# Sample attention handles two cached pieces per visit of TensorE instead of one, in a one-core decoder step

## The chip, the cores and the metric

The kernel runs on one core of a Trainium2 chip. The metric is the device time in microseconds of one execution. Three runs of the kernel before gave 2272.2 us in the median (2270.72 to 2273.8).

## The reference

One layer of a hybrid decoder, for 512 prompt tokens and 8 sample sequences of 4 new tokens each, model width 2048, everything in float32:

```python
h = rmsnorm(x); [q | k | v | u] = h @ w_in
A = dilated sliding-window attention on (q, k, v)     # 16 heads x 64
B = multi-scale causal pooling on u
x = x + concat(A, B) @ w_out
x = x + SwiGLU(rmsnorm(x));  y = rmsnorm(x)
```

The part that matters here is attention for the sample tokens, where each sequence has a cache of 2048 keys and values:

```python
kcat = jnp.concatenate([ck, k], axis=1); vcat = jnp.concatenate([cv, v], axis=1)
kg, vg = kcat[:, idxc], vcat[:, idxc]                 # gathered by stride
logits = jnp.einsum('bthd,btkhd->bhtk', q, kg) * scale + bias
p = jax.nn.softmax(logits, axis=-1)
out = jnp.einsum('bhtk,btkhd->bthd', p, vg)
```

Of the cached positions only 896 can be reached by any of the four queries (`NK` = 896, seven tiles of 128); with the 32 new tokens there are `NL` = 928 columns of logits, held as two halves of `HL` = 464.

## The kernel before

Everything is transposed: channels on partitions, the 544 tokens (512 prompt, 32 sample) along the free dimension. A projection is computed one tile of 128 output channels at a time: 16 steps over the input channels (`kt`), in each of which `mm3` (L193 to L199) issues six matmuls of 272 columns, since every float32 product is made of three products of rounded high and low parts. The weights come through a stream (`Stream`, L115): a DMA of 256 KB for four steps (L129), rounded by ScalarE (L143) and subtracted by VectorE (L148) ahead of use.

Attention is woven into the projections. `project` yields after every step, and after each yield `tick` (L765) is called, which may run a piece of prompt attention and a piece of sample attention; what these issue lands in program order between the six matmuls of one step and those of the next. `clock["d"]` counts the ticks. There are 48 for each of the eight head pairs `hp` (q, k and v tiles), from 48 on, and then 16 for each of eight u tiles.

Sample attention is a generator per group `g` of four heads, `sample_steps` (L574), appended when `hp` = 1, 3, 5, 7 is done, so it can first run in ticks 97, 193, 289 and 385. For each half `kh` of the keys it issues one bias matmul (`btH`), then for each of four `bl` (one sequence of each half of the batch) four matmuls L588, one per 32 output partitions, which read a piece of cached keys, and then two more bias matmuls (`btL`, `selR`) and a bare `yield`. Then come the softmax (VectorE, ScalarE, with bare yields between) and two rounds of transposes. After that for each `j` of seven cached tiles of values and one of new values there are four matmuls L635. Each group so reads eight pieces of keys and seven of values.

The pieces (928, 864 or 1024 KB) lie in `NBUF` = 3 buffers. `load_piece` (L406) is called after the matmuls of a piece, and issues the DMA (L413) of the piece three further on, into the buffer just read; so that DMA waits for those matmuls. It goes out on SyncE's queue (SP), which issues in program order, and which the weights of the projections (L129) and all small transfers use too.

What sets the pace is the counter `clock["s"]`. In each tick the loop at L777 runs the generator on as long as the counter is below `(d - 96) * 64 / 352`. A `yield 1` adds one to the counter and the loop goes on; a bare `yield` (r = 0) ends the loop for this tick; the end of the generator (r = -1) takes it off the queue and also adds one. While no group is queued the target goes on rising. After the sixth u tile's start (tick 480) whatever is left is run to its end.

Of the kernel before, what the change touches and what calls it, by code (L numbers as in the profile page):

```python
# [163 lines left out]
def program(ctx, tc, a):  # L164
    nc = tc.nc
# [128 lines left out]
    with pool("st", side="right") as sp:  # L294
# [41 lines left out]
        for u in range(NU):  # L336
            wq, wk = ws.take(), ws.take()
            for i in range(UW):
# [12 lines left out]
                if kt == 8:  # L351
                    fps = pS.tile([P, 512], F32, tag="S", name="fps")
                    for h in range(2):
                        nc.tensor.matmul(fps[h * 32:h * 32 + H, :320], rb33, c33[:, 320 * h:320 * h + 320], start=True,
                                         stop=True)
# [29 lines left out]
    loaded = deque()  # L385
# [11 lines left out]
    qz = [at.tile([P, 2, 160], F32, name=f"qz{i}") for i in range(4)]  # L397
# [8 lines left out]
    def load_piece():  # L406
        n = state["n"]
        if n < len(pieces) and len(loaded) < NBUF:
            src = pieces[n]
            t = kvp[0].tile([P, PIECE], F32, tag="kv", name="kv", bufs=NBUF)  # L410
            w = src.shape[1] * src.shape[2]
            v = t[:, :w].rearrange("p (c k) -> p c k", c=src.shape[1])
            dma(v, src)  # L413
            loaded.append(v)
            state["n"] = n + 1
# [158 lines left out]
    def sample_steps(g):  # L574
        ps = pS.tile([P, 2, 512], F32, tag="samp", name="SS")
        par = [(2 * g + hpl) % 4 for hpl in range(2)]
        for kh in range(2):
            o = ps[:, kh, :HL]
            ks = slice(kh * HL, (kh + 1) * HL)
            nc.tensor.matmul(o, btH[:, g], bohR[:, ks], start=True, stop=False, skip_group_check=True)  # L580
            if kh:
                for c in range(4):
                    nc.tensor.matmul(ps[32 * c:32 * c + 32, 1, NK1:HL], qd[par[c // 2]][:, c % 2],
                                     kn[par[c // 2]], start=False, stop=False, skip_group_check=True)
            for bl in range(4):
                kv = loaded.popleft()
                for c in range(4):
                    nc.tensor.matmul(ps[32 * c:32 * c + 32, kh, :kv.shape[2]],  # L588
                                     qz[par[c // 2]][:, c % 2, 32 * bl:32 * bl + 32], kv[:, c],
                                     start=False, stop=False, skip_group_check=True)  # L590
                load_piece()
                yield 1
            nc.tensor.matmul(o, btL[:, g], bohR[:, ks], start=False, stop=False, skip_group_check=True)
            nc.tensor.matmul(o, selR, browR[:, ks], start=False, stop=True, skip_group_check=True)
            yield
        yield
        sm = at.tile([P, 4], F32, name="sm", tag="sms", bufs=2)
        prob = at.tile([P, NL], F32, name="sprob", tag="sprob")
        nc.vector.tensor_reduce(sm[:, 0:1], ps[:, :, :HL], axis=AX.XY, op=ALU.max)
        nc.vector.tensor_scalar(sm[:, 1:2], sm[:, 0:1], -1.0, None, op0=ALU.mult)  # L600
        yield
        nc.scalar.activation(prob.rearrange("p (a b) -> p a b", a=2), ps[:, :, :HL], AF.Exp, bias=sm[:, 1:2],
                             accum_out=sm[:, 2:3])
        yield
        yield
        nc.vector.reciprocal(sm[:, 3:4], sm[:, 2:3])
        nc.vector.tensor_scalar(prob, prob, sm[:, 3:4], None, op0=ALU.mult)
        yield
        yield
        ptr = at.tile([P, NJ, P], F32, name="ptr", tag="ptr")  # L610
        for half in range(2):
            pt = pS.tile([P, 4, P], F32, tag="T", name="tps")
            for jj in range(4):
                j = 4 * half + jj
                if j < NJ:
                    nc.tensor.transpose(pt[:, jj], prob[:, j * P:(j + 1) * P], ident)
                else:
                    nc.tensor.transpose(pt[:NS, jj], prob[:, j * P:], ident)
            if half == 0:
                nc.vector.tensor_copy(ptr[:, :4], pt)  # L620
            else:
                nc.vector.tensor_copy(ptr[:, 4:], pt[:, :3])
                nc.vector.tensor_copy(pt7[:NS], pt[:NS, 3])
            yield
        pot = pS.tile([P, 2, 512], F32, tag="samp", name="SO")
        po = pot[:, 0]
        for j in range(NJ + 1):
            kv = loaded.popleft() if j < NJ else None
            for c in range(4):
                l = (ptr[:, j] if j < NJ else pt7)[:, 32 * c:32 * c + 32]  # L630
                if j < NJ:
                    r = kv.rearrange("p c (b f) -> p c b f", b=DB)[:, c // 2, 4 * (c % 2):4 * (c % 2) + 4]
                else:
                    r = vn[par[c // 2]][:, None, :].to_broadcast([P, 4, P])
                nc.tensor.matmul(po[32 * c:32 * c + 32, :].rearrange("p (b f) -> p b f", b=4), l, r,  # L635
                                 start=(j == 0), stop=(j == NJ), skip_group_check=True)
            if j < NJ:
                load_piece()
            yield 1
        vm = at.tile([P, 4, P], F32, name="vm", tag="vm")  # L640
        yield
        nc.vector.tensor_mul(vm, po.rearrange("p (b f) -> p b f", b=4), vmask)
        for _ in range(3):
            yield
        for b in range(4):
            nc.tensor.matmul(pot[:, 1, :64], vm[:, b], sel64, start=(b == 0), stop=(b == 3))
        m = at.tile([P, 64], F32, name="ms", tag="ms")
        nc.vector.tensor_copy(m, pot[:, 1, :64])
        for hpl in range(2):
            dma(mixd[2 * g + hpl][:, SEQ:], m[:, 32 * hpl:32 * hpl + 32])  # L650
        yield
# [93 lines left out]
    def run(gen, n=10 ** 6):  # L745
        r = 0
        for _ in range(n):
            r = next(gen, -1)
            if r == -1:
                return -1  # L750
        return r or 0
# [8 lines left out]
    clock = {"d": SPAN, "s": 0, "p": 0}  # L760
# [4 lines left out]
    def tick(lo, hi):  # L765

        clock["d"] += 1
        d = clock["d"]
        if d < S_FROM and d % 3 == 0:
            run(setup, 1)  # L770
        if d == S_FROM:
            run(setup)
        while prompt and clock["p"] < (d - lo) * P_STEPS / (hi - lo):
            clock["p"] += 1
            if run(prompt[0], 1) < 0:
                prompt.pop()
        while samples and clock["s"] < (d - S_FROM) * S_STEPS / (S_TO - S_FROM):  # L777
            r = run(samples[0], 1)
            if r < 0:
                samples.popleft()  # L780
            elif r == 0:
                break
            clock["s"] += 1

    for hp in range(8):
        for out in (q_out, k_out, v_out):
            acc = accv
            if hp:
                acc = acc_tile()
                for _ in project(acc):  # L790
                    tick(SPAN * hp, SPAN * hp + SPAN - 2)
            if hp or out is v_out:
                out(hp, acc)
        finish(prompt)
        clock["p"] = 0
        spread(hp)
        prompt.append(prompt_steps(hp))
        if hp % 2:
            samples.append(sample_steps(hp // 2))
# [26 lines left out]
    for n, ft in enumerate(u_order):  # L826
# [15 lines left out]
        for i, _ in enumerate(project(acc)):  # L842
            tick(8 * SPAN, 8 * SPAN + 3 * KT)
            if pools and run(pools[0], 1) < 0:
                pools.popleft()
            if staged and i % 2 and (n > 6 or i > 5):
                mix_in(*staged.popleft())
                mix_load()
# [183 lines left out]
    for n, nt in enumerate(nts):  # L1032
        load_x2(n + 1)
        acc = acc_tile()
        for u in range(NU):
            wh, wl, _ = ws.next()
# [7 lines left out]
            for i in range(UW):  # L1044
                j = UW * u + i
# [167 lines left out]
    for ci, (c0, n) in enumerate(chunks[:-1]):  # L1213
        groups = parts.pop(ci)
        ahead = load_g(ci + 1)
        for nt in range(KT):
# [3 lines left out]
            for u in range(n // UW):  # L1220
                if ci == nt == 0:
                    run(g0, 10 ** 6 if u == n // UW - 1 else 2)
                wh, wl, _ = ws2.next()
# [24 lines left out]
    for h in range(2):  # L1248
        c = slice(h * HALF, (h + 1) * HALF)
        for nt in range(KT):  # L1250
# [6 lines left out]
            for i in range(UW):  # L1257
                j = nt % 4 * UW + i
# [77 lines left out]
```

## Time and profile before

| | us |
|---|---|
| median of three runs | 2272.2 |
| the profiled execution | 2272.66 |
| its span, first to last instruction | 2270.9 |
| TensorE matmuls busy | 2236.9 (99%) |
| weight loads busy | 2143.0 (94%) |
| VectorE busy | 1387.8 (61%) |
| ScalarE busy | 851.9 (38%) |

The profiled execution has 1.8 us outside its span. Busy times are of one engine each and overlap; a matmul's end is modelled, so that consecutive matmuls overlap on the page and the time between two starts is what a matmul costs. A float32 matmul of the sample part shows as two records, so four of them stand as x8.

### The profile page before, as it was taken

How to read it: one execution, taken by the hardware profiler on the slowest of the kernel's cores; microseconds unless marked ns; L12 is line 12 of the kernel's file. 1: busy time of each engine (PE TensorE's matmuls, PEld its weight loads, DVE VectorE, ACT ScalarE, POOL GpSimd, SP SyncE). 2: the span in 40 equal slices, each digit the busy share in tenths (PEclk: the TensorE clock that was granted, in tenths of full speed). 3: DMA queues.
4: the chain of work that ended last, by engine and by line, in shares of the span. 5: the costliest groups of instructions: out<-in, count | busy, mean ns of one | idle time of the engine just before them, and what ended most of it. 6: DMA issues, size and time to landing. Idle time of an engine off the chain costs nothing.

```text
span 2270.9 us, 43394 instructions
## 1 busy us (share of the span) xinstructions
PE 2236.9 (99%) x17540; PEld 2143.0 (94%) x17540; DVE 1387.8 (61%) x2659; ACT 851.9 (38%) x1621; POOL 3.6 (0%) x28
## 2 busy tenths in 40 slices
PE   8999999999999999999999999999999999999997
PEld 8878787879999999999999999999999999999997
DVE  7644445476544688877878878887785333323256
ACT  6322222223333454444444444444444222222235
POOL 0000000000000000000000000000000000000000
PEclk9999999999999999999999999999999999999998
DMA  6666656676444432342343343333335533332233
GB/s 195 198 220 203 224 200 233 204 207 156 139 126 135 149 124 92 115 132 96 111 132 100 107 132 106 105 128 112 104 109 168 165 116 114 123 103 89 85 112 108
DMA packets 158693, 316.71 MB, mean 139 GB/s; under 512 B 28747, under 2 KB 34011, under 8 KB 154908
## 3 DMA queue, kind: packets, MB, share of 16 engines
q1 hardware_dynamic: 158112, 313.77, 43.4%
q8 instruction: 137, 2.24, 0.4%
q14 instruction: 64, 0.52, 0.1%
q10 hardware_dynamic: 380, 0.18, 0.0%
HBM read 284.32 MB, written 29.56 MB: 138 GB/s over the span
## 4 chain that ended last, share of the span: by engine, by line
PE 95%; DVE 2%; DMA 1%; ACT 1%; issue 1%; SPq 0%; DVEq 0%; ACTq 0%
PE acc L197 16%; PE acc L198 15%; PE acc L199 15%; PE X L973 8%; PE X L972 8%; PE X L974 8%; PE Z L973 4%; PE Z L972 4%; PE Z L974 4%; PE Y L973 2%; PE Y L972 2%; PE Y L974 2%; PE SO L635 1%; PE SS L588 1%; PE S L519 1%; PE O L565 1%
## 5 line engine op out<-in xcount | busy, mean ns | idle before, releaser
L973 PE MATMUL X<-bL,whi 128*128 128x272 f32 x1408 | 409.9, 291 | 0.1
L972 PE MATMUL X<-bH,whi 128*128 128x272 f32 x1408 | 406.8, 289 | 2.7 <-ACT whi L949 1.9
L974 PE MATMUL X<-bH,wlo 128*128 128x272 f32 x1408 | 407.3, 289 | 0.7 <-DVE wlo L915 0.6
L143 ACT ACTIVATE whi<-raw 128x512 fp32r<-128x512 f32 x352 | 218.3, 628 | 472.5 <-PE acc L198 438.4
L198 PE MATMUL acc<-gL,whi 128*128 128x272 f32 x1280 | 371.7, 290 | 0.4 <-DVE gL L1144 0.4
L197 PE MATMUL acc<-gH,whi 128*128 128x272 f32 x1280 | 368.7, 288 | 1.3 <-ACT gH L1143 1.3
L199 PE MATMUL acc<-gH,wlo 128*128 128x272 f32 x1280 | 369.1, 288 | 0.0
L949 ACT ACTIVATE whi<-s 128x512 fp32r<-128x512 f32 x352 | 213.7, 631 | 334.6 <-DVE s L935 153.7
L197 PE MATMUL acc<-hH,whi 128*128 128x272 f32 x992 | 305.0, 307 | 6.5 <-ACT whi L143 6.5
L148 DVE TENSOR_TENSOR wlo<-raw,whi 128x512 fp32r<-128x512 f32 x352 | 236.3, 685 | 84.9 <-issue 78.4
L199 PE MATMUL acc<-hH,wlo 128*128 128x272 f32 x992 | 288.0, 290 | 0.0
L198 PE MATMUL acc<-hL,whi 128*128 128x272 f32 x992 | 286.5, 289 | 0.0
L972 PEld LDWEIGHTS X<-bH,whi 128*128 128x128 f32 x1408 | 266.5, 189 | 3.2 <-ACT whi L949 2.1
L974 PEld LDWEIGHTS X<-bH,wlo 128*128 128x128 f32 x1408 | 266.1, 189 | 1.2 <-DVE wlo L915 1.2
L973 PEld LDWEIGHTS X<-bL,whi 128*128 128x128 f32 x1408 | 265.2, 188 | 0.3 <-DVE bL L1083 0.3
L915 DVE TENSOR_TENSOR wlo<-s,whi 128x512 fp32r<-128x512 f32 x352 | 241.6, 686 | 22.3 <-ACT whi L949 22.2
L197 PEld LDWEIGHTS acc<-hH,whi 128*128 128x128 f32 x992 | 187.7, 189 | 64.3 <-issue 55.3
L197 PEld LDWEIGHTS acc<-gH,whi 128*128 128x128 f32 x1280 | 241.4, 189 | 1.7 <-ACT gH L1143 1.7
L199 PEld LDWEIGHTS acc<-gH,wlo 128*128 128x128 f32 x1280 | 241.0, 188 | 0.2 <-DVE wlo L148 0.2
L198 PEld LDWEIGHTS acc<-gL,whi 128*128 128x128 f32 x1280 | 240.2, 188 | 0.6 <-DVE gL L1144 0.6
L915 DVE TENSOR_TENSOR wlo<-a,whi 128x512 fp32r<-128x512 f32 x264 | 181.3, 687 | 35.5 <-ACT whi L949 30.5
L1232 DVE TENSOR_TENSOR x<-acc,x 128x544 f32<-128x544 f32 x64 | 46.4, 725 | 255.5 <-PE acc L199 255.5
(221 smaller groups left out, 4468.2 us busy)
## 6 DMA issues: line engine op xcount, KB each, us to landing
a<-w_gate SPq DMA_DIRECT2D x176, 256.0 KB, 4.6
a<-w_up SPq DMA_DIRECT2D x176, 256.0 KB, 4.8
raw<-w_down SPq DMA_DIRECT2D x176, 256.0 KB, 2.8
raw<-w_in SPq DMA_DIRECT2D x128, 256.0 KB, 3.9
kv<-cv SPq DMA_DIRECT2D x28, 1024.0 KB, 6.5
raw<-w_out SPq DMA_DIRECT2D x64, 256.0 KB, 3.4
kv<-ck SPq DMA_DIRECT2D x16, 928.0 KB, 5.0
kv<-ck SPq DMA_DIRECT2D x16, 864.0 KB, 4.7
```

The source lines that it names most:

```text
L143: nc.scalar.activation(hi[:, :n], t[:, :n], AF.Copy)
L148: nc.vector.tensor_sub(lo[:, :n], t[:, :n], hi[:, :n].bitcast(F32))
L197: nc.tensor.matmul(o, wh[:, i, :], xh[:, kt, c], start=start, stop=False)
L198: nc.tensor.matmul(o, wh[:, i, :], xl[:, kt, c], start=False, stop=False)
L199: nc.tensor.matmul(o, wl[:, i, :], xh[:, kt, c], start=False, stop=stop)
L519: nc.tensor.matmul(ps[s][:, :w], q[r, c], x[r, :w], start=(k == 0), stop=(k == 2))
L915: nc.vector.tensor_sub(lo, x, hi.bitcast(F32))
L949: nc.scalar.activation(hi, x, AF.Copy)
L972: nc.tensor.matmul(o, wh[:, j], bh[:, k], start=first, stop=False, skip_group_check=True)
L973: nc.tensor.matmul(o, wh[:, j], bl[:, k], start=False, stop=False, skip_group_check=True)
L974: nc.tensor.matmul(o, wl[:, j], bh[:, k], start=False, stop=last, skip_group_check=True)
L1232: nc.vector.tensor_add(two(x2[:, nt]), acc[:, :, :HALF], two(x2[:, nt]))
```

## The change

In the key loop two pieces are taken from the queue, their eight matmuls are issued, then two loads are issued, then the generator yields 2. In the value loop a yield comes after every second tile and is worth 2; the load still follows each tile. The pacing loop adds `r`, whatever it is, in place of one.

```diff
-            for bl in range(4):
-                kv = loaded.popleft()
-                for c in range(4):
-                    nc.tensor.matmul(ps[32 * c:32 * c + 32, kh, :kv.shape[2]],
-                                     qz[par[c // 2]][:, c % 2, 32 * bl:32 * bl + 32], kv[:, c],
-                                     start=False, stop=False, skip_group_check=True)
-                load_piece()
-                yield 1
+            for bl in range(0, 4, 2):
+                kvs = [loaded.popleft() for _ in range(2)]
+                for b, kv in enumerate(kvs):
+                    for c in range(4):
+                        nc.tensor.matmul(ps[32 * c:32 * c + 32, kh, :kv.shape[2]],
+                                         qz[par[c // 2]][:, c % 2, 32 * (bl + b):32 * (bl + b) + 32], kv[:, c],
+                                         start=False, stop=False, skip_group_check=True)
+                for _ in kvs:
+                    load_piece()
+                yield 2
...
             if j < NJ:
                 load_piece()
-            yield 1
+            if j % 2:
+                yield 2
...
             elif r == 0:
                 break
-            clock["s"] += 1
+            clock["s"] += r
```

## Rows read from the trace of the kernel before

**Rows 1.** The page, part 1: busy us (share of the span) and instructions.

```profile
PE 2236.9 (99%) x17540; PEld 2143.0 (94%) x17540; DVE 1387.8 (61%) x2659; ACT 851.9 (38%) x1621; POOL 3.6 (0%) x28
```

**Rows 2.** The page, part 4: chain that ended last, shares by engine.

```profile
PE 95%; DVE 2%; DMA 1%; ACT 1%; issue 1%; SPq 0%; DVEq 0%; ACTq 0%
```

**Rows 3.** Waits of PE, 90 to 545 us: first and last of three.

```profile
PE tps L616 <- DVE vn L505: 1.4, 1, 1.4
...
PE tps L616 <- DVE ptr L620: 0.7, 1, 0.7
```

**Rows 4.** Instructions that read the cached pieces: ns min/median/max, starts, forms.

```profile
L588 PE MATMUL SS<-kv,qz x256: 526/550/577, 95.8 to 473.6; 128*32 128x464 f32 x64, 128*32 128x432 f32 x64
...
L635 PE MATMUL SO<-kv,ptr x224: 592/592/617, 159.4 to 519.8; 128*32 128x512 f32 x112
```

**Rows 5.** Timeline of PE, a lone key visit: start us, us, instruction.

```profile
113.39 0.29 PE L199 MATMUL acc<-hH,wlo 128*128 128x272 f32 x1
113.60 0.98 PE L588 MATMUL SS<-kv,qz 128*32 128x464 f32 x8
114.52 0.40 PE L197 MATMUL acc<-hH,whi 128*128 128x272 f32 x1
114.75 0.29 PE L198 MATMUL acc<-hL,whi 128*128 128x272 f32 x1
```

**Rows 6.** Timeline of PE, a group's first key visits, ticks 193, 289, 385.

```profile
209.99 1.25 PE L588 MATMUL SS<-kv,qz 128*32 128x464 f32 x8
211.17 0.40 PE L197 MATMUL acc<-hH,whi 128*128 128x272 f32 x1
...
323.18 2.03 PE L588 MATMUL SS<-kv,qz 128*32 128x464 f32 x16
325.14 0.40 PE L197 MATMUL acc<-hH,whi 128*128 128x272 f32 x1
...
435.81 2.03 PE L588 MATMUL SS<-kv,qz 128*32 128x464 f32 x16
```

**Rows 7.** Timeline of PE, value tiles 0 and 1, then 2 (first group).

```profile
159.36 1.92 PE L635 MATMUL SO<-kv,ptr 128*32 128x512 f32 x16
161.22 0.39 PE L197 MATMUL acc<-hH,whi 128*128 128x272 f32 x1
...
162.92 1.07 PE L635 MATMUL SO<-kv,ptr 128*32 128x512 f32 x8
163.91 0.39 PE L197 MATMUL acc<-hH,whi 128*128 128x272 f32 x1
```

**Rows 8.** Timeline of SP's DMA issues: start us, us, instruction.

```profile
160.49 3.88 SPq L413 DMA_DIRECT2D kv<-cv  x3
...
324.75 0.86 SPq L413 DMA_DIRECT2D kv<-ck  x2
...
437.52 1.88 SPq L803 DMA_DIRECT2D rcnt<-rcnt  x1
...
439.99 2.06 SPq L413 DMA_DIRECT2D kv<-ck  x3
```

**Rows 9.** Issue to landing: at 160.49; both at 324.75; two at 439.99.

```profile
DMA to landing us min/median/max: 5.0/5.0/5.0
...
DMA to landing us min/median/max: 5.1/5.9/6.7
...
kv<-ck SPq DMA_DIRECT2D x2, 864.0 KB, 7.8
```

**Rows 10.** Stage 5 to 10 us: engines, PEclk, DMA share, GB/s.

```profile
5.00:10.00 5.00, 3.54 (x14) 3.31 (x15) 3.32 (x6) 3.70 (x6) 0.00 (x0) 1.00 1.00 366
```

**Rows 11.** Stages around two idle times of PE, columns as in Rows 10.

```profile
155.00:160.00 5.00, 4.04 (x34) 3.24 (x38) 3.38 (x10) 0.09 (x1) 0.00 (x0) 1.00 0.20 55
...
582.00:586.00 4.00, 3.70 (x17) 3.71 (x18) 1.50 (x4) 0.01 (x1) 0.00 (x0) 0.57 0.52 134
```

**Rows 12.** Timeline of PE, the idle time ahead of 582.

```profile
581.54 0.39 PE L736 MATMUL pout<-zH,wpH 128*128 128x272 f32 x1 [2.91 <-ACT zH L708]
```

## The prediction

> **What bounds the kernel now.** I read the page's busy times first, then the chain, then PE's waits in the stretch where the change acts, and last the timelines of PE and SP around single visits. PE is busy 99% of the span [rows 1] and 95% of the chain that ended last is PE [rows 2]. Between 90 and 545 us, where all sample attention lies, PE waits for other engines three times, 1.4 us at the longest [rows 3]. So in this stretch a microsecond that PE saves is a microsecond off the end, and one that it waits is a microsecond on it. No wait for a cached piece is among the three: with three buffers and one piece per visit, loads are hidden today.
>
> **What is removed.** The matmuls stay the same [rows 4]; what goes is leaving and re-entering the projection. A lone key visit: from the last projection matmul ahead of it to the second one behind it 114.75 - 113.39 = 1.36 us [rows 5]. Without the visit that would be two matmul spacings, at 2236.9 / 17540 = 0.128 us each [rows 1], so the visit costs 1.11. What a second piece in the same visit costs is there too, since the pacing already makes some doubles: a group's first visit takes 211.17 - 209.99 = 1.18 us alone and 325.14 - 323.18 = 1.96 doubled [rows 6], so the second piece costs 0.78, and a merge saves 0.33. For values the double takes 161.22 - 159.36 = 1.86, the single 163.91 - 162.92 = 0.99 [rows 7]; the second tile costs 0.87, and the single with the key visit's head and tail (0.20) 1.19, a saving of 0.32. I take 0.33.
>
> How many merges there are follows from the pacing. The target at tick d is (d - 96) x 2/11. Before, a group adds 16 for its visits and one at its end, so the counter stands at 17, 34, 51 when groups 1, 2, 3 start at ticks 193, 289, 385, where the targets are 17.6, 35.1 and 52.5: one visit, two, two. The trace has x8 at 209.99 and x16 at 323.18 and 435.81 [rows 6]: the arithmetic holds. Carried through all ticks, TensorE leaves the projection 8 + 8 + 7 + 7 times for keys and 4 x 7 times for values (the first value visit is a double), 58 in all. After, it is 4 + 3 + 3 + 2 for keys and 4 x 4 for values, 28. Thirty are gone: 30 x 0.33 = 9.9 us. Between 7.8 (if ten stand beside prompt matmuls that switch the array anyway and save only 0.12) and 11 (the last key visits of groups 2 and 3 also share a tick with the bias matmuls behind them).
>
> **What is added: bursts that three buffers can't feed.** The end of a generator is r = -1, and the counter now adds r: it goes back by one where it went forward. A group is worth 15, and groups 1 to 3 start with the counter at 15, 30, 45 against the same targets. Tick 193: 15 to 17 to 19, two visits, four pieces at once. Tick 289: 30 to 34, four pieces, then the bare yield ends the tick; at 290 34 is below 35.3, two more. Tick 385: 45 to 49, four; tick 386: 49 to 53 against 52.7, four more, eight pieces with one projection step between. With three pieces in the buffers, the fourth is only requested when the first has been used, and TensorE, which works in order, stands until it lands; behind the waiting matmul are all projections, and nothing else can run on it.
>
> Take t = 0 where the first piece is done; the second and third take 0.78 each, so the fourth is wanted at 1.56. At tick 289 the load goes out at 324.75 [rows 8], 0.4 after 323.18 + 1.18 (SP is just done with a weight load), and lands 5.1 later, the next, issued 0.4 later, in 6.7 [rows 9].
> - Tick 193: lands at 5.5, wait 5.5 - 1.56 = 3.9. Bounds 3.4 (issued at once, landing 5.0) to 4.5.
> - Ticks 289/290: the fourth is done at 6.3, then some 1.8 of bias matmuls and one projection step (estimate). The fifth landed at 7.5 and runs from 8.1 to 8.9; the sixth queues behind it, 0.885 MB at 366 GB/s with the DMA engines full [rows 10] = 2.4, and lands at 9.9. End 10.7 against 2.3 + 1.8 + 1.6 = 5.7 without waits: 5.0. Bounds 3.9 to 8.
> - Ticks 385/386: here SP is held up by the small loads of the pooling part (1.88 us at the last) and the piece goes out only at 439.99 [rows 8], 3.0 after t = 0; the two behind it landed in 7.8 [rows 9]. So the fourth lands at about 9, the fifth and sixth at 11.6 and 12.8, the seventh, requested at 9.9 when the fourth is done, at 15.2, the eighth, requested at 12.4, at some 17.3 (4.9 to land). End 18.1 against 7.3: wait 10.8. Bounds 8 to 14.
> - Values: the softmax takes some ten ticks during which the counter lags, so in every group tiles 0 and 1 come in one tick (150 in group 0) as before, and two ticks later tile 2, now with tile 3. Tile 3 is requested when tile 0 is done: issued 160.49, landing after 5.0, at 165.5 [rows 8, 9]. Tile 2 is done at 163.91 [rows 7]. Wait 1.6; with a landing of 7.8 it is 4.4. I take 1.8, near the row for this very load, four times: 7.2. Bounds 4.8 to 17.6.
>
> Sum of waits 26.9, bounds 20 to 44. Pairs elsewhere are 9 to 12 ticks apart, 7 us or more, and find their pieces: no wait. Two loads in a row also stand ahead of weight loads on SP; these are requested some six units of 24 matmuls (3.1 us each by rows 1) ahead, and I cost that at nothing; if the cover fails it is the third rival.
>
> **The clock after a wait.** After an idle time of 2.91 us [rows 12] the granted clock was 0.57 over the next four [rows 11], close to the lower of the two levels (1.2 GHz); that lost 0.43 x 4 = 1.7 us. After 1.4 us of idle it stayed at 1.00 [rows 3, 11]. Four waits here are longer than 2.9 (ticks 193, 289, two at 385/386), but part of the slow time lies inside the next wait. I take two: 3.4; bounds 0 and 6.8. The Trainium skill ("TensorE: Matmul & The Clock Gate", section on HAM oscillation) warns that DMA waits between bursts of matmuls send the clock down every time; the row at 582 agrees, the one at 155 does not. By that rule alone the sum has eight such losses in place of two; what that makes is the second rival.
>
> The Trainium skill ("DMA: Bandwidth & Descriptors", section Bandwidth) gives 6.15 us for 1 MB, from another issuing engine; the row here has 5.0 with landing included. By the page, an estimate, seven waits would each be about 1 us longer; I go by the row.
>
> **Sum.** -9.9 + 26.9 + 3.4 = +20.4 on the profiled execution's 2272.7, which is 0.5 above the median of 2272.2: 2293 us. Ends: -11 + 20 + 0 = +9 (2281) and -7.8 + 44 + 6.8 = +43 (2315). Starting softmax earlier in the prompt's cycle may add or drop a wait like that of L616, 1.4 us either way; I leave it out of the sum.
>
> **Rivals.**
> 1. Faster, 2262: the merges bring 9.9 and the third buffer is enough. Place: ticks 193, 289, 385. It decides as soon as a burst needs no more than three pieces, as in group 0, whose pairs come at 97, 108, 120 and 130. For it: today no wait for a piece shows [rows 3]. Against: the counter arithmetic, which names the two x16 rows right. 0.08.
> 2. The clock falls at all eight waits: 8 x 1.7 = 13.6 in place of 3.4, 2303. For it the row at 582; against it the 1.4 us wait, near in size to those of the value tiles. 0.12.
> 3. The weights starve: ten loads go past SP around tick 386 and weight loads queue behind up to 3 MB, 8 us at 366 GB/s [rows 10]; ScalarE's rounding comes late and TensorE waits again, some 5 us there and 5 over the other bursts: 2303. Against: two units are rounded ahead, and SP's loads stand idle while TensorE does. 0.08.
> 4. A draw: waits about 10 us because pieces land in some 3 us when the weights' stream pauses. Against: the landing rows are 5.0 and more. 0.06.
>
> The forecast has 0.66. About 0.2% (4.5 us) is what a measurement here can tell from no change: faster 0.08, same 0.06, slower 0.86. The range 2278 to 2306 takes in the forecast down to below its low end, and rivals 2 and 3 at their estimates; it leaves out the fast rival, most of the draw and the upper tail.
>
> **What will show it.** Right: L588 groups of x32 at the first tick of groups 1 to 3, with PE idle inside them and a DMA kv named as releaser, some 4, 5 and 11 us; 1 to 3 us inside each group's third and fourth value tile; group 3 over about 33 ticks earlier; a granted clock below 1 in the slices around 440 us. Wrong: waits of PE on kv under 10 us in total, bursts no longer than x16, or the time growing after 545 us.

## The result, and the profile after

The changed kernel took 2301.97 us in the median of four runs (2298.7 to 2305.13), the kernel before 2272.93 beside it: a ratio of 1.0129 (95% interval 1.011 to 1.0148), 29 us slower. The profiled execution took 2299.65 us, its span 2297.8; that is 26.9 us over the span of before, and this is the difference that the profile has to explain. It is one execution's: the mean granted clock was 0.992 in it and 0.988 to 0.990 in the other three, so what the clock takes differs from run to run.

The busy times and the chain of the changed kernel (columns as before):

```profile
PE 2235.8 (97%) x17540; PEld 2145.5 (93%) x17540; DVE 1385.4 (60%) x2659; ACT 850.3 (37%) x1621; POOL 3.6 (0%) x28
...
PE 92%; DMA 3%; DVE 3%; issue 1%; ACT 1%; SPq 0%; DVEq 0%; ACTq 0%
```

(PE is TensorE's matmuls, DVE VectorE, ACT ScalarE, SP SyncE.) Against [rows 1] TensorE is busy for about the same time, with the same number of matmuls, in a longer span, and DMA has grown from 1% to 3% of the chain [rows 2]. What TensorE waits for between 90 and 560 us (us in total, times, longest):

```profile
PE SS L589 <- DMA kv<-ck: 19.5, 5, 7.4
PE SO L637 <- DMA kv<-cv: 6.3, 4, 1.9
PE tps L618 <- DVE sm L523: 2.5, 2, 1.4
PE tps L618 <- DVE vn L505: 1.4, 1, 1.4
```

Beside [rows 3] there are nine waits for cached pieces, 25.8 us together, none of which was there. The key waits stand where the counter puts bursts, the four value waits where tile 3 now follows tile 2 at once. The timeline of PE at the starts of groups 1, 2 and 3 (start, duration, instruction, idle time ahead of it and what ended it):

```profile
210.42 2.81 PE L589 MATMUL SS<-kv,qz 128*32 128x464 f32 x24
217.39 0.99 PE L589 MATMUL SS<-kv,qz 128*32 128x464 f32 x8 [4.16 <-DMA kv<-ck]
...
218.65 0.43 PE L198 MATMUL acc<-hL,whi 128*128 128x272 f32 x1
...
328.11 2.81 PE L589 MATMUL SS<-kv,qz 128*32 128x464 f32 x24
336.00 1.77 PE L589 MATMUL SS<-kv,qz 128*32 128x464 f32 x8 [5.08 <-DMA kv<-ck]
...
341.24 3.09 PE L589 MATMUL SS<-kv,qz 128*32 128x432 f32 x16
...
461.00 1.77 PE L589 MATMUL SS<-kv,qz 128*32 128x464 f32 x8 [7.42 <-DMA kv<-ck]
...
469.19 0.93 PE L589 MATMUL SS<-kv,qz 128*32 128x432 f32 x8 [0.68 <-DMA kv<-ck]
472.33 0.93 PE L589 MATMUL SS<-kv,qz 128*32 128x432 f32 x8 [2.20 <-DMA kv<-ck]
...
484.00 0.63 PE L618 MATMUL tps<-ident,sprob 128*128 128x128 f32 x4 [1.14 <-DVE sm L523]
...
493.54 1.06 PE L637 MATMUL SO<-kv,ptr 128*32 128x512 f32 x8 [1.93 <-DMA kv<-cv]
```

Three pieces run (x24), then TensorE stands until the fourth lands; in [rows 6] the same places had one or two pieces and no wait. Read the durations too: the fourth piece takes 0.99 us at 217.39 but 1.77 at 336.00 and 461.00, two pieces at 341.24 take 3.09 where a double was 2.03, and a projection matmul behind a wait takes 0.43 in place of 0.29. The clock has gone down. The stages behind the waits (columns as in Rows 10; a clock of 0.50 is the lower of TensorE's two levels, 1.2 GHz, and a value between has part of each):

```profile
217.00:221.00 4.00, 3.61 (x20) 2.85 (x21) 0.00 (x0) 0.00 (x0) 0.00 (x0) 0.67 1.02 427
221.00:223.00 2.00, 2.00 (x15) 1.98 (x15) 0.72 (x2) 0.00 (x0) 0.00 (x0) 0.80 0.93 391
...
336.00:345.00 9.00, 9.00 (x45) 3.85 (x46) 0.00 (x0) 0.00 (x0) 0.00 (x0) 0.52 0.68 238
...
461.00:464.00 3.00, 3.00 (x10) 0.77 (x10) 0.00 (x0) 0.00 (x0) 0.00 (x0) 0.50 0.99 396
464.00:469.00 5.00, 4.52 (x32) 2.26 (x31) 0.00 (x0) 0.00 (x0) 0.00 (x0) 0.64 0.56 185
...
494.00:499.00 5.00, 5.00 (x31) 4.46 (x24) 2.58 (x7) 0.00 (x0) 0.00 (x0) 0.66 1.00 423
```

The time missing to a clock of 1.00 is 0.33 x 4 + 0.20 x 2 = 1.7 us, 0.48 x 9 = 4.3, 0.50 x 3 + 0.36 x 5 = 3.3 and 0.34 x 5 = 1.7: 11.0 in all.

Whether this is the whole difference is read from two marks, VectorE's reads of the sixth u tile, which ends at tick 480 (it doesn't start there) and behind all sample attention, and of the first w_out tile, first in the kernel before, then in the changed one:

```profile
545.39 0.72 DVE L670 TENSOR_TENSOR u<-acc,rinv 128x544 f32<-128x544 f32 x1 [4.51 <-PE acc L199]
593.38 0.72 DVE L1060 TENSOR_TENSOR x<-acc,xr 128x544 f32<-128x544 f32 x1 [1.98 <-PE acc L199]
```

```profile
575.46 0.72 DVE L673 TENSOR_TENSOR u<-acc,rinv 128x544 f32<-128x544 f32 x1 [4.10 <-PE acc L199]
622.13 0.72 DVE L1063 TENSOR_TENSOR x<-acc,xr 128x544 f32<-128x544 f32 x1 [1.98 <-PE acc L199]
```

At the first mark the changed kernel is 30.1 us late, of which 0.8 was there before any sample attention (the first v tile is read at 95.71 in place of 94.96), so the stretch with the change took 29.3 longer. With the merges' forecast 9.9 off, the waits' 25.8, the clock's 11.0 and 1.8 more for waits on VectorE (3.9 in place of 2.1) the sum is 28.7. Behind that stretch 3.2 us come back, which the change didn't aim at: 1.3 up to the second mark, a stretch with the pooling output in it, where the kernel before waited 2.9 us and then ran at 0.57 [rows 11] and the changed one waited 2.1 and stayed at 1.00 (612 to 616 us), and 1.9 in smaller steps from there to the end.

### The profile page after: what moved, and what is told of

The parts are those of the page before. It is cut to its first block, busy times and chain, and to the rows that moved or that the text cites. A ratio compares the mean times of both kernels' runs of the same rounds, so it can differ in the third digit from the quotient of the medians.

```text
span 2297.8 us, 43381 instructions
## 1 busy us (share of the span) xinstructions
PE 2235.8 (97%) x17540; PEld 2145.5 (93%) x17540; DVE 1385.4 (60%) x2659; ACT 850.3 (37%) x1621; POOL 3.6 (0%) x28
## 4 chain that ended last, share of the span: by engine, by line
PE 92%; DMA 3%; DVE 3%; issue 1%; ACT 1%; SPq 0%; DVEq 0%; ACTq 0%
PE acc L197 15%; PE acc L199 15%; PE acc L198 15%; PE X L976 7%; PE X L975 7%; PE X L977 7%; PE Z L976 4%; PE Z L975 4%; PE Z L977 4%; PE Y L976 2%; PE Y L975 2%; PE Y L977 2%; DMA kv<-ck 1%; PE SO L637 1%; PE S L519 1%; PE SS L589 1%
```

## The experiments

Two questions: whether the bursts made the loss (theory A) or the pair itself (B), and whether the part that the waits don't make up is the clock (C) or nothing that costs (D). Each experiment was timed against the kernel before on the same chip.

### The end of a group adds one again

```diff
-            clock["s"] += r
+            clock["s"] += r if r > 0 else 1
```

> The changed kernel, but the end of a group adds one to the counter, as before. Theory A (bursts: the end that takes one away makes groups 1 to 3 start in bursts of four to eight pieces, which three buffers can't feed): bursts of key pieces are two at a time, so the waits on key pieces fall from 19.5 us to the one at ticks 385/388, three ticks apart, some 4.5 us with 2 us of slow clock behind it; the waits on value tiles stay at some 6.3; 26 merges at 0.33 us bring 8.6. About 2277 us, 4 above the kernel before, 25 below the changed one. Theory B (the pair itself: two loads in a row on SP and longer visits hold up the weights, and the counter is harmless): stays near 2300.

Measured: 2280.88 us, 1.0031 of before (1.002 to 1.0043). Of the 29 us, 20.5 are gone with this one line, and all pairs are still there; B, which had 2300, is out. What is left, 8.6 us by the medians, is the pairs' own with three buffers, where two of them come two or three ticks apart. Waits for pieces in it:

```profile
PE SO L637 <- DMA kv<-cv: 8.2, 4, 4.8
PE SS L589 <- DMA kv<-ck: 3.8, 1, 3.8
```

The one key wait is the expected one at ticks 385/388. One value wait was 4.8, nearly three times the size I gave it: SP stood at the output of v and a weight load, so the piece went out at 381.15, 1.7 us after tile 0 was done, and it took 7.1 us to land. Both long waits left the clock low, which the 7 us and 6 us around and behind them show:

```profile
388.00:395.00 7.00, 6.69 (x33) 4.76 (x33) 0.88 (x2) 0.00 (x0) 0.00 (x0) 0.53 0.89 322
450.00:456.00 6.00, 5.46 (x27) 3.63 (x27) 0.28 (x1) 0.00 (x0) 0.00 (x0) 0.50 0.90 331
```

That is 0.47 x 7 + 0.50 x 6 = 6.3 us, where I had put 2. The profiled execution, 2284.05 us and the slowest of seven, is 7 over the forecast of 2277: the clock makes up 4.3 of it, the waits (12.0 for 10.8) 1.2, and the rest I didn't trace.

### One piece per visit, and the end takes one away

```diff
-            clock["s"] += 1
+            clock["s"] += r
```

This is the kernel before with that line of the change alone.

> The kernel before, one piece per visit, but the counter adds r as in the changed kernel (so the end of a group takes one away). Theory A: bursts of three pieces at tick 193, six at 289/290, eight at 385/386; the first finds its pieces, the other two wait as in the changed kernel (5.1 and 10.3 us) with some 7 us of slow clock, the value tiles don't wait; ten merges bring 3.3: about 2292 us. Theory B: no pairs, so no loss; 2270.

Measured: 2294.63 us, 1.0094 (1.0081 to 1.0108). So 22 of the 29 us come without a single pair. The burst of three at tick 193 ran through (the fourth piece, three ticks later, waited 1.16), and the waits at 289 (4.3 us) and at 385/386 (6.6, 1.1 and 1.7) are close to those of the changed kernel (5.1 and 10.3). At 289:

```profile
322.31 2.81 PE L588 MATMUL SS<-kv,qz 128*32 128x464 f32 x24
329.41 1.78 PE L588 MATMUL SS<-kv,qz 128*32 128x464 f32 x8 [4.29 <-DMA kv<-ck]
```

### Matmuls that fill the waits

```diff
+    FILL = {(1, 0, 3): 30, (2, 0, 3): 38, (3, 0, 3): 58, (3, 1, 3): 12, (3, "v", 3): 10}
+    def filler(n):
+        for _ in range(n):
+            nc.tensor.matmul(acc[:, 0, HALF:HALF + 240], hH[:, 0, :P], hH[:, 0, :240], start=True, stop=True,
+                             skip_group_check=True)
...
                 for b, kv in enumerate(kvs):
+                    filler(FILL.get((g, kh, bl + b), 0))
...
             kv = loaded.popleft() if j < NJ else None
+            filler(FILL.get((g, "v", j), 0))
```

The filler writes, with `start=True`, into the accumulators' bank while projections are under way there. This kernel doesn't compute the layer's values and serves for its time alone.

> The changed kernel, with matmuls of 240 columns that nothing reads (30, 38, 58, 12 and 10 of them, some 0.11 us each) put in front of the pieces that TensorE waits for, a little less than each wait, so that TensorE stays busy while it waits. They add work, and leave the pieces' landing as it is. Theory C (the part of the loss that the waits don't make up, some 8 us of it, is the slower clock after each long wait): the granted clock stays at 1.00 in these stretches, the waits shrink to what the filler leaves, and the time falls by 5 to 9 us to some 2293 to 2297. Theory D (the clock costs nothing, since the slow stretches are followed by waits that absorb them): no change, 2302 within 2 us, or slower by what the filler overshoots.

Measured: 2296.85 us, 1.0104 (1.009 to 1.0118): more work, and 5 us less than the changed kernel in the medians, at the near end of what C expected; the two intervals against before overlap by 0.0008, so the size is less sure than the clock rows. These are, at two of the places shown above:

```profile
217.00:221.00 4.00, 4.00 (x34) 3.71 (x31) 1.32 (x3) 0.00 (x0) 0.00 (x0) 1.00 0.96 376
336.00:345.00 9.00, 8.87 (x78) 6.09 (x71) 3.91 (x14) 1.47 (x5) 0.00 (x0) 1.00 0.94 339
```

In the nine microseconds in which the changed kernel started 45 matmuls, this one, a little further on in the work, started 78. Not all came back: with TensorE at full speed the next pieces were waited for instead (the fourth value tile of group 2 waited 2.7 where it had waited 1.3), and the clock still fell, for 3.4 us each, at 462 and 489, where waits of 1.8 and 2.1 were left. In the two profiled executions waits for pieces and filler together take 30.1 us (11.3 and 18.8) in place of 25.8, and the clock 3.4 in place of 11.0: 3.3 less, and they are 3.5 apart. C holds, D not.

### Four buffers

```diff
-    NBUF = 3
+    NBUF = 4
...
-        vT[hp] = at.tile([P, TOK], F32, name="vT", tag="vT", bufs=2)
+        vT[hp] = at.tile([P, TOK], F32, name="vT", tag="vT")
...
-        vm = at.tile([P, 4, P], F32, name="vm", tag="vm")
+        vm = at.tile([P, 4, P], F32, name="vm", tag="sprob")
...
-        m = at.tile([P, SEQ], F32, name="mp", tag="mp")
+        m = at.tile([P, SEQ], F32, name="mp", tag="ql")
...
-    vmask = at.tile([P, 4, P], F32, name="vmask")
+    vmask = at.tile([P, 8], F32, name="vmask")
```

> The changed kernel with four buffers for the cached pieces in place of three; the room comes from tiles that share space (the masked product with the probabilities, the prompt output with a rounded query, one v tile in place of two, a mask of 8 columns read by broadcast), which should cost nothing. Theory A: no wait at tick 193 and none in the value tiles, 2 to 3 us at 289/290, 8 to 9 at 385/386 where the loads go out late and eight pieces are wanted, with one or two stretches of slow clock: about 2278 us. Theory B: no better than the changed kernel, 2300.

Measured: 2279.07 us, 1.0027 (1.0018 to 1.0036). One more buffer takes back 22 of the 29 us that the changed schedule had lost. Tick 193 and the value tiles don't wait; what is left is at 289/290 and 385/386, where six and eight pieces are wanted: 2.2 us and 5.0 us, six waits in all. The second is well under the 8 to 9 expected, and the ten microseconds from 442 to 452, behind its first wait, ran at 0.51; so the forecast of 2278 is near in its sum rather than in its parts. The profiled execution, 2275.58 us, is also the fastest of the ten.

### The kernel before with four buffers

The same edits on the kernel before.

> The kernel before with the fourth buffer and the shared tiles of e4, nothing else. Both theories: one piece per visit never waits with three buffers, so the fourth buffer and the sharing change nothing, 2272 within 2 us. A gain or loss here would have to be taken off e4, e6 and e7.

Measured: 2273.76 us, 1.0003 (0.9994 to 1.0012). Where nothing waits for a piece, a buffer buys nothing, so what e4 and the next one gain is not the sharing's.

### Pairs, four buffers, and the end adds one

The edits of e1 and e4 together. Theory E, named here and in the next expectation, is that a pair costs something that the waits don't show, such as two loads in a row on SP, so that a merge brings less than 0.33 us.

> The changed kernel with four buffers, and the end of a group adds one. Theory A: at most four pieces are wanted within five microseconds, so no wait but perhaps 1 to 2 us at ticks 385/388, no slow clock, 26 merges at 0.33: about 2264 us. Theory E: 2269 to 2272.

Measured: 2263.57 us, 0.9962 (0.9949 to 0.9974): 9.4 us faster than before, with 26 merges. TensorE's waits between 90 and 560 us are those of the kernel before and no others:

```profile
PE tps L618 <- DVE vn L505: 1.4, 1, 1.4
PE pout L740 <- DVE ptr L622: 0.8, 1, 0.8
PE tps L618 <- DVE ptr L622: 0.7, 1, 0.7
```

### Pairs spread out, three buffers

On the kernel of e1:

```diff
                 yield 2
+                if kh == bl == 0:
+                    for _ in range(5):
+                        yield
...
             if j % 2:
                 yield 2
+            if j == 1:
+                for _ in range(5):
+                    yield
```

> The kernel of e1 (pairs, the end of a group adds one), three buffers, with five bare yields behind a group's first key visit and five behind its first value visit, so that the next pair comes some six ticks (5 us) later. Theory A: no wait on a piece longer than about 1 us, no slow clock before 560 us, 26 merges at 0.33 bring 8.6: about 2264 to 2266 us. Theory E (a pair costs something that the waits don't show, as two loads in a row on SP, and the merges bring less than their 0.33): 2269 to 2272.

Measured: 2272.95 us, 1.0000 (0.9992 to 1.0009), some 8 us over the forecast. One piece broke it, the second value pair of group 3:

```profile
501.97 1.07 PE L640 MATMUL SO<-kv,ptr 128*32 128x512 f32 x8
506.86 1.93 PE L640 MATMUL SO<-kv,ptr 128*32 128x512 f32 x8 [3.83 <-DMA kv<-cv]
```

The two pieces requested at 496.5 took 11.2 us to land in the median, not 5: 60 KB of pooling state in and 60 KB out, moved in many small packets, had gone out on the same queue 2 to 3 us ahead of them. The issues from 490 to 498 us (KB each, us to landing) and a stage in which the DMA engines are 0.81 busy and move 47 GB/s:

```profile
kv<-cv SPq DMA_DIRECT2D x2, 1024.0 KB, 11.2
st<-state SPq DMA_DIRECT2D x1, 60.0 KB, 6.6
sp<-uc SPq DMA_DIRECT2D x1, 60.0 KB, 8.8
...
500.00:502.00 2.00, 2.00 (x21) 1.85 (x20) 0.56 (x1) 0.36 (x1) 0.00 (x0) 1.00 0.81 47
```

The wait of 3.8 and the slow clock behind it (0.51 from 507 to 512) make up about 6 of the 8 us. The rest, against the trace of e6, which has the same merges: 0.5 for one more wait on a piece, and 3.3 from the sixth u tile on, where this kernel waited 3.4 us at the pooling output in place of 2.4 and two stretches at the lower clock, from 580 and from 785 us, were 6.8 us long in place of 3.4. That it is the state's traffic is read from these rows and not tried. The time alone, 2272.95, would fit theory E better than A; but the losses stand in the rows, and e6 has the pairs and the gain.

### Four pieces per visit, four buffers

```diff
-            for bl in range(0, 4, 2):
-                kvs = [loaded.popleft() for _ in range(2)]
+            for bl in range(0, 4, 4):
+                kvs = [loaded.popleft() for _ in range(4)]
...
-            if j % 2:
-                yield 2
+            if j % 4 == 3:
+                yield 4
```

On the kernel of e6; the key loop yields 4 as well.

> The kernel of e6 with four pieces per visit instead of two, the visits 22 ticks (some 17 us) apart: 16 visits for the sample attention in place of 32, 16 more merges. If a merge saves 0.33 whatever the size of the visit, 5 us less than e6, about 2259 us; against it, four loads (4 MB) follow each other on SP, and where two visits are less than about 15 us apart (values: 12 ticks, 9 us) the last pieces come late by 1 to 3 us a group, which takes all of it back: 2263 to 2270.

Measured: 2262.48 us, 0.9955 (0.9942 to 0.9969): the fastest of all, but 1 us under e6 and not 5, and the intervals overlap. No piece was waited for. Two marks tell where the rest went, VectorE's read of the sixth u tile and of the first w_out tile, in e6 and then in e7:

```profile
537.48 0.72 DVE L674 TENSOR_TENSOR u<-acc,rinv 128x544 f32<-128x544 f32 x1 [4.50 <-PE acc L199]
585.29 0.72 DVE L1064 TENSOR_TENSOR x<-acc,xr 128x544 f32<-128x544 f32 x1 [1.98 <-PE acc L199]
```

```profile
532.70 0.72 DVE L674 TENSOR_TENSOR u<-acc,rinv 128x544 f32<-128x544 f32 x1 [4.49 <-PE acc L199]
582.80 0.72 DVE L1064 TENSOR_TENSOR x<-acc,xr 128x544 f32<-128x544 f32 x1 [1.97 <-PE acc L199]
```

At the first e7 is 4.8 us ahead (1.0 of it from an earlier start of the projections, and with 1.35 us lost to a new wait in prompt attention, so the merges bring what they should), at the second 2.5. Between them lies the pooling output, whose wait for ScalarE was 2.4 us in e6 and 4.1 in e7, and the clock behind it was lower for longer (0.72 from 574 to 580 in e6, 0.51 from 569 to 576 in e7). That wait also grew, from 2.9 to 3.5 us, in the kernel before with four buffers, which has no other schedule; so I can't call it a consequence of the earlier arrival.

## Why the prediction was right, and which term was too small

The forecast was 2293 us, 20 us slower; the changed kernel took 2302 in the median and 2299.65 in the profiled execution. Term by term:

- **What bounds.** Right: TensorE's waits went onto the end nearly one for one. To the sixth u tile the changed kernel lost 29.3 us where waits, clock and merges add up to 28.7. That only 26.9 are left at the end is chance: the 3.2 that came back behind it lie outside sample attention, and no term of the forecast had them.
- **The merges.** Right in kind, a little small. From the first v tile, read at 94.96 in both, to the sixth u tile e6 is 7.9 us quicker than the kernel before (537.48 for 545.39) for 26 merges: 0.30 each against 0.33, so 9.1 for thirty in place of 9.9. The traces have the visits as counted: 30 and 28 before, 12 and 16 in the changed kernel.
- **The counter.** Right, and it is the main cause: taking that one line back removes 20.5 us, putting it alone into the kernel before costs 22. It costs because three buffers can't feed its bursts: with four, e4 has the same line and 22 us less.
- **The waits.** 26.9 forecast, 25.8 found. Tick 193: 3.9 and 4.16; 289/290: 5.0 and 5.08, but the forecast had 3.9 at the fourth piece and the rest at the sixth, and all of it was at the fourth, whose load took 6.3 us in place of 5.1, so that the sum is right by luck; 385/386: 10.8 and 7.42 + 0.68 + 2.20 = 10.3; values 7.2 and 6.3.
- **The clock.** This is the term that was mis-sized: 3.4 forecast, some 11.0 found, and outside its bounds (0 to 6.8). The step that failed is "part of the slow time lies inside the next wait. I take two". I priced a loss with the one stretch of [rows 11], 1.7 us, and thought of the projection alone. In the changed kernel the burst goes on behind the wait, at the lower clock, and at 336 the slow stretch was nine microseconds and cost 4.3; that the one comes of the other is not shown. And a fourth loss followed two waits of 1.14 and 1.93 us close together at 484 and 494, which I had counted as too short. With 7.6 more for this term, 1.1 less for the waits on pieces, 1.8 for those on VectorE (left out of the sum, as 1.4 either way) and 0.8 for the merges the forecast's 20.4 becomes 29.5, where 29.3 were found. e3 shows that the clock was low because TensorE stood: kept busy, it stayed at 1.00 at two of the four places.
- **The rule on the clock.** The Trainium skill's warning ("TensorE: Matmul & The Clock Gate", HAM oscillation) comes nearer in the sum than my use of one row, and not in the count: of the nine waits on pieces, the three of 4.16 us and more were each followed by the lower clock, and the one of 1.93 at 494, ten microseconds after one of 1.14 on VectorE, too; the three lone value waits of 1.3 to 1.7 us were not. As in the second rival, all eight would have been 13.6; the trace has four stretches, two of them long, and 11.0.
- **The rivals.** No weights were late: between 90 and 560 us TensorE waited for no rounded weight. The fast rival is a time that can be had, with one more buffer and the end that adds one: e6 ran in 2263.6, where it stood at 2262.

## What to carry to other kernels

When several steps of a paced side task are put into one visit, count the pieces wanted within one load's landing time, not on the average: here, with three buffers, a pair every eleven ticks was free, two pairs two or three ticks apart cost 1.3 to 4.8 us, and four to eight pieces at once cost 4 to 10 us each time. Look at every value that a pacing counter can be given, the end's included; one sign cost twice as much as the change could bring. And price a wait of TensorE at more than its length: here 25.8 us of waiting took 11 us more in a lower clock behind it.

## What was not expected of the hardware

The time that the clock takes did not go by the length of the wait alone: behind 4.16 us of waiting 1.7 us were lost, behind 5.08 us 4.3, behind 7.42 us 3.3. What else decides it no run here shows. And a load's landing time moved between 4.7 us (the kernel before) and 12.0 us (e5) for the same megabyte, the longest with two transfers of 60 KB in small packets ahead of it.
